# Turning layer 0's attention probabilities in 32 by 32 squares on VectorE, with the squares changing places through DRAM

## The chip, the cores and the metric

The kernel runs on one core of a Trainium2 chip. A core has five engines, each with a queue of its own that is worked through in order: TensorE (matrix products, PE in the profile, with its weight loads as PEld), VectorE (DVE), ScalarE (ACT), GpSimd (POOL) and SyncE (SP). SP and ACT also issue DMAs from their queues (SPq and ACTq in the profile), and 16 DMA engines carry them out. The metric is the device time of one execution in microseconds, the median of several runs.

## The reference

Two decoder layers over 272 tokens (16 learned meta tokens and a sequence of 256), with 16 heads of 128 features. Layer 0 is forgetting attention, layer 1 stick-breaking attention, each with a squared-ReLU MLP behind it. The change is in layer 0's attention:

```python
def forgetting_attention(q, k, v, cum_logf):
    scale = HEAD_DIM ** -0.5
    outs = []
    for qs, qe in query_blocks(q.shape[1]):
        s = jnp.einsum('bqhd,bkhd->bhqk', q[:, qs:qe], k[:, :qe]).astype(jnp.float32) * scale
        s = s + cum_logf[:, :, qs:qe, None] - cum_logf[:, :, None, :qe]
        ...
        p = jax.nn.softmax(s, axis=-1).astype(v.dtype)
        outs.append(jnp.einsum('bhqk,bkhd->bqhd', p, v[:, :qe]))
    return jnp.concatenate(outs, axis=1)
```

The blocks of queries are the 16 meta tokens and two blocks of 128. The softmax runs over keys, and the product with v sums over keys.

## The kernel before

Activations lie feature-major: a feature on a partition, the 272 tokens along the free dimension. Almost all of the time is in `gemm_group`, which computes 512 output features: 16 chunks of 128 input features, four blocks of 128 output features. To keep float32 accuracy at the speed of the float32r type, each operand is split in a high and a low part, and three products (high by high, high by low, low by high) are summed in PSUM. The weights are split on the way: SP loads `raw` blocks (L207), ACT makes the high part `whi` (L218), DVE the low part `wlo` (L219). One weight block is 256 input features by 512; there are four buffers each for `raw`, `whi` and `wlo`, so the splits can run up to four blocks ahead of TensorE, and eight blocks make a group.

In layer 0 the loop at L421 goes over four groups `g` of four heads. Each does three `gemm_group` calls, for q, k and v, and the attention work is woven between the products of the next of these calls:

- L460 to L477: for each head `j`, the scores of both query blocks are computed (L466, and L467 by `by_parts`, L394), added to the decays on DVE (L470), made into exponentials on ACT (L473) and divided by their sums (L475, L477). They stand in `s`, queries on partitions, keys along the free dimension: 144 keys for the first block of queries, 272 for the second.
- L479 to L489: the same for the meta tokens, in `s0`.
- L492 to L507: to be summed over keys, the probabilities must have the keys on partitions. For each pair of heads `pr`, and each head `i` in it, three squares of 128 by 128 are turned on TensorE (L501, a product with the identity), into the PSUM tile `pp`. Two of them are split into a high and a low part `p0` (`split`, L376 on ACT and L377 on DVE), the third goes to `p1` whole (L506).
- L510 to L517: two more squares, the corners `pk_sm` (packed on POOL, L412) and `s0`, are turned on TensorE (L511, L512) and copied to `pm_sb`.
- L519: the `gemm_group` of v. Then v is turned to token-major (`token_major`, L384), and the products with p follow: `weighted` (L397, whose products are at L394) for `p0` and L539 for `p1`.

Each engine's order is made when the program is built: the framework lays the instructions of a queue in an order by a simulated timeline (the argument at L865), and puts a semaphore wait wherever an instruction uses what another engine or a DMA makes. `placed_behind` only pins one instruction behind another on TensorE. An engine whose next instruction waits does nothing else, and that holds for a DMA issue too: an issue on ACT's queue that waits holds up the activations behind it.

The tiles `raw`, `q2` and `p0` of the attention come from three buffers named `pp` in the pool `att`; `p1` shares two buffers of the pool `tmp`.

The kernel already has one trip through DRAM on ACT's queue: in group 0 the forget gates' running sums go to `f_dram` (L370), and are read back from there as `fqm_sb` (L372) and, once in every group, `fk` (L445).

Of the kernel before, what the change touches and what calls it, by code (L numbers as in the profile page):

```python
# [9 lines left out]
F32 = mybir.dt.float32  # L10
# [5 lines left out]
P = 128  # L16
# [17 lines left out]
def yoco_kernel(ctx: ExitStack, tc: tile.TileContext, hT_in, gains, b_f, w_f, w_qkv0, w_o0, w_up, w_dn,  # L34
                w_kv, w_q1, w_o1, g_row, out):
    nc = tc.nc
# [8 lines left out]
    att = ctx.enter_context(tc.tile_pool(name="att", bufs=2))  # L45
    pacc = ctx.enter_context(tc.tile_pool(name="pacc", bufs=4, space=bass.MemoryType.PSUM))
    patt = ctx.enter_context(tc.tile_pool(name="patt", bufs=4, space=bass.MemoryType.PSUM))
# [14 lines left out]
    ident = const.tile([P, P], F32, name="ident")  # L62
# [117 lines left out]
    def placed_behind(product, *others):  # L180

        for o in others:
            tc.add_manual_dep(product.ins, o.ins.name, mybir.DependencyInfo(mybir.DependencyClass.NoSync,
                                                                            mybir.DependencyReason.DATA))
# [136 lines left out]
    fq_sb = const.tile([P, 2, NC], F32, name="fq_sb")  # L321
    fqm_sb = const.tile([P, 4], F32, name="fqm_sb")
    f_dram = tc.dram_tile([NC, T], F32, name="f_dram")

    def load_gates():
        nc.scalar.dma_start(bf_sb, b_f)

        wf_sb = att.tile([P, NC, NC], F32, tag="v_sb", name="wf_sb")
        wf = att.tile([P, NC, 2 * NC], F32, tag="v_sb", name="wf")
        nc.scalar.dma_start(wf_sb, w_f)  # L330
        nc.vector.memset(wf[:, :, NC:], 0.0)
        nc.vector.tensor_tensor(out=wf[:, :, :NC], in0=wf_sb, in1=g_sb[:, G_A0, :].unsqueeze(2).to_broadcast([P, NC, NC]), op=ALU.mult)
        both = att.tile([P, P], F32, tag="pk", name="both")[:, :32]
        nc.vector.tensor_tensor(out=both, in0=ident[:, :32], in1=ident[:, 32:64], op=ALU.add)
        for i in (2, 3):
            nc.vector.tensor_tensor(out=both, in0=both, in1=ident[:, 32 * i:32 * i + 32], op=ALU.add)
        both = both[:, :NC]
        return wf, both
# [35 lines left out]
    def split(hl, src):  # L374

        nc.scalar.activation(hl[:, 0], src, AF.Copy)  # L376
        nc.vector.tensor_tensor(out=hl[:, 1], in0=src, in1=hl[:, 0].bitcast(F32), op=ALU.subtract)  # L377

    def token_major(vT, pr, t0, label):

        pv = patt.tile([P, 2, 2, P], F32, tag="patt", name=f"pv_{label}")
        for i in range(2):
            for b in range(2):
                nc.tensor.transpose(pv[:, i, b, :], vT[:, 2 * pr + i, t0 + b * P:t0 + b * P + P], ident)  # L384
        v0 = att.tile([P, 2, 2, P], F32R, tag="v_sb", name=f"v0_{label}")
        v1 = tmp.tile([P, T], F32, tag="u2", name=f"v1_{label}")[:, :2 * P].rearrange("p (i d) -> p i d", i=2)
        split(v0, pv[:, :, 0, :])
        nc.scalar.copy(v1, pv[:, :, 1, :])
        return v0, v1

    def by_parts(out, a, b, start, stop=False):

        for k, (i, j) in enumerate(((0, 0), (0, 1), (1, 0))):
            product = nc.tensor.matmul(out, a[i], b[j], start=start and k == 0, stop=stop and k == 2)  # L394
        return product

    def weighted(po, v0, p0, i):  # L397

        return by_parts(po[:, i, :], [v0[:, k, i, :] for k in range(2)], [p0[:, k, i, :] for k in range(2)], i == 0)

    def packed(src, label):

# [12 lines left out]
    def put_split(sp, h, nh, t, n, src):  # L415
        hi, lo = (x[:, h:h + nh, t - sp.t0:t - sp.t0 + n] for x in (sp.hi, sp.lo))
        nc.scalar.activation(hi, src, AF.Copy)
        nc.vector.tensor_tensor(out=lo, in0=src, in1=hi.bitcast(F32), op=ALU.subtract)

    ao = Split("o0", 0)  # L420
    for g in range(4):  # L421
# [24 lines left out]
        s = att.tile([P, 4, 416], F32, tag="s", bufs=1, name=f"s_{g}")  # L446
# [15 lines left out]
        for j in range(4):  # L462
            h = 4 * g + j
            ps = patt.tile([P, 512], F32, tag="patt", name=f"ps_{h}")
# [14 lines left out]
        ps = patt.tile([P, 512], F32, tag="patt", name=f"ps0_{g}")  # L479
# [11 lines left out]

        pps = []  # L492
        for pr in range(2):
            p0 = att.tile([P, 2, 2, 256], F32R, tag="pp", bufs=3, name=f"p0_{g}_{pr}")
            p1 = tmp.tile([P, T], F32, tag="relu", name=f"p1_{g}_{pr}")[:, :2 * P].rearrange("p (i q) -> p i q", i=2)
            last = None
            for i in (1, 0):
                j = 2 * pr + i
                pp = patt.tile([P, 512], F32, tag="patt", name=f"pp_{4 * g + j}")
                for b, o in ((2, 144 + P), (1, 144), (0, 0)):  # L500
                    product = nc.tensor.transpose(pp[:, b * P:(b + 1) * P], s[:, j, o:o + P], ident)  # L501
                    if last is not None:
                        placed_behind(product, last)
                    last = product
                split(p0[:, :, i, :], pp[:, :2 * P])
                nc.vector.tensor_copy(p1[:, i, :], pp[:, 2 * P:3 * P])  # L506
            pps.append((p0, p1))  # L507


# [18 lines left out]
        po = patt.tile([P, 512], F32, tag="patt", name=f"pom_{g}")  # L528
# [5 lines left out]
        for pr in range(2):  # L534
            (v0, v1), (p0, p1) = token_major(vT, pr, 0, f"0_{g}_{pr}"), pps[pr]
            po = patt.tile([P, 2, 256], F32, tag="patt", name=f"po0_{g}_{pr}")
            for i in range(2):
                weighted(po, v0, p0, i)
                nc.tensor.matmul(po[:, i, P:], v1[:, i, :], p1[:, i, :], start=False, stop=i == 1)  # L539
            ends = po.rearrange("p i (c q) -> p (i c) q", c=2)[:, :, P - M:]  # L540
            nc.vector.tensor_tensor(out=ends, in0=ends, in1=own[:, 4 * pr:4 * pr + 4], op=ALU.add)
            put_split(ao, 4 * g + 2 * pr, 2, M, S, po)
# [78 lines left out]
    for g in range(4):  # L621
        kT = att.tile([P, 4, T], F32, tag="kT", bufs=1, name=f"kT1_{g}")
        gemm_group(w_kv[2 * g], xc, 0, lambda m, acc: evac_kv(m, acc, kT))
        q = qT1[g]
# [33 lines left out]
        for pr in range(2):  # L658
# [3 lines left out]
            for i in range(2):  # L662
                j = 2 * pr + i
                product = by_parts(pa[:, i, :], [k0[:, k, j, :] for k in range(2)],
                                   [x[:, 4 * g + j] for x in (ao.hi, ao.lo)], True, True)
            for i in range(2):
                j = 2 * pr + i
# [26 lines left out]
            product = nc.tensor.matmul(pb[:, :, :144], ntri_r, e_lo[:, :, 256:400], start=False, stop=True)  # L694
# [8 lines left out]
        ps = []  # L703
        for pr in range(2):
            zp = z[:, 2 * pr:2 * pr + 2, :400]
            nc.scalar.activation(zp, zp, AF.Exp)
            p0 = att.tile([P, 4, T], F32R, tag=("kT", "qT")[pr], bufs=(1, 4)[pr], name=f"p01_{g}_{pr}")
            p0 = p0.rearrange("p h t -> p (h t)")[:, :1024].rearrange("p (a i q) -> p a i q", a=2, i=2)
# [11 lines left out]
        for pr in range(2):  # L720
            v0, v1 = token_major(vT, pr, 0, f"1_{g}_{pr}")
            po = patt.tile([P, 2, 256], F32, tag="patt", name=f"po1_{g}_{pr}")
            for i in range(2):
                j = 2 * pr + i
                product = weighted(po, v0, ps[pr], i)
                if j == 0:
                    placed_behind(nc.tensor.matmul(pv[:, P:P + 64], vc_sb, zc, start=True, stop=True), product)
                    nc.scalar.copy(own, pv[:, P:P + 64].rearrange("p (h q) -> p h q", h=4))
                nc.tensor.matmul(po[:, i, 112:], v1[:, i, :], z[:, j, 256:400], start=False, stop=i == 1)  # L729
            nc.vector.tensor_tensor(out=po[:, :, 240:], in0=po[:, :, 240:], in1=own[:, 2 * pr:2 * pr + 2], op=ALU.add)  # L730
            put_split(ao, 4 * g + 2 * pr, 2, M, S, po)
# [141 lines left out]
```

## Time and profile before

| | |
|---|---|
| median of 3 runs | 2289.8 us (2289.29 to 2289.85) |
| the profiled execution, its own time | 2290.0 us |
| its span in the profile | 2288.3 us |
| granted TensorE clock | 1.0 throughout |
| layer 0's attention, groups 0 to 3 | about 24 to 341 us of the span |
| one group of four heads, groups 1 to 3 | 79.30 us each |
| transposes L501 | 48, 270 to 273 ns each |

A row of a timeline has the start and the length in microseconds, the engine, the line of the kernel, the operation, what it writes and reads, and how many instructions it merges; idle time of the engine before it stands in brackets with what ended it. A row of the stretches has, for each engine, the busy time and the number of instructions, then the granted clock, the DMA engines' busy share and what they moved. A row of DMA issues ends with the size of one transfer and the median time from issue to landing.

### The profile page before, as it was taken

To read this page: it belongs to the slowest core of one execution; us is meant where nothing else is said; L and a number is where in the kernel's file an instruction comes from. 1 tells how busy PE (TensorE), PEld (TensorE's weight loads), DVE (VectorE), ACT (ScalarE), POOL (GpSimd) and SP (SyncE) were. 2 spreads that over 40 slices of the span, in tenths; PEclk is the share of its full clock that TensorE was granted. 3 is DMA by queue.
4 is the path that set the end of the run, shared out by engine and by line. 5 is a ranking of instruction groups with operands and counts; after the bars stand their busy time and mean duration, and the time that the engine had idled before them with its cause. 6 is when DMAs were issued, how large, how long until landed. Compare 5 with 4: busy or idle time off the path is not lost.

```text
span 2288.3 us, 44927 instructions
## 1 busy us (share of the span) xinstructions
PE 2281.3 (100%) x18994; PEld 2272.9 (99%) x18994; DVE 1321.5 (58%) x1858; ACT 1066.4 (47%) x1479; POOL 44.7 (2%) x72
## 2 busy tenths in 40 slices
PE   9999999999999999999999999999999999999999
PEld 9999999999999999999999999999999999999998
DVE  7666565654455455455566666666555555555555
ACT  6444444444354344344444455555543543544554
POOL 1010000000000000000000000000000000000001
PEclk9999999999999999999999999999999999999999
DMA  7545545555555555555555544456556566565564
GB/s 242 171 162 162 181 156 171 175 185 176 180 170 184 180 171 185 175 184 176 174 187 191 177 148 148 154 174 203 186 192 201 186 195 203 185 202 192 186 201 142
DMA packets 116283, 412.60 MB, mean 180 GB/s; under 512 B 13537, under 2 KB 15473, under 8 KB 116081
## 3 DMA queue, kind: packets, MB, share of 16 engines
q1 hardware_dynamic: 113760, 406.29, 54.8%
q10 hardware_dynamic: 2320, 3.43, 0.4%
q8 instruction: 149, 2.44, 0.4%
q14 instruction: 54, 0.43, 0.1%
HBM read 407.55 MB, written 2.11 MB: 179 GB/s over the span
## 4 chain that ended last, share of the span: by engine, by line
PE 99%; DMA 0%; ACT 0%; DVE 0%; issue 0%; POOL 0%; POOLq 0%; SPq 0%; DVEq 0%
PE acc L188 96%; PE po L394 0%; PE pv L384 0%; PE ps L394 0%; PE pza L394 0%; PE pp L501 0%; DMA raw<-w_qkv 0%; PE pzb L668 0%; PE po L729 0%; PE ps L466 0%; PE po L539 0%; DMA hT<-hT_in 0%; ACT whi L218 0%; PE pf L345 0%; DVE wlo L219 0%
## 5 line engine op out<-in xcount | busy, mean ns | idle before, releaser
L219 DVE TENSOR_TENSOR wlo<-raw,whi 128x1024 fp32r<-128x1024 f32 (+1 forms) x773 | 929.1, 1218 | 728.9 <-ACT whi L218 721.8
L218 ACT ACTIVATE whi<-raw 128x1024 fp32r<-128x1024 f32 (+1 forms) x773 | 796.8, 1050 | 978.4 <-PE acc L188 931.4
L188 PE MATMUL acc<-x_m,whi 128*128 128x272 f32 (+1 forms) x4096 | 643.2, 282 | 0.0
L188 PE MATMUL acc<-x_u,whi 128*128 128x272 f32 (+1 forms) x3968 | 626.1, 282 | 0.0
L188 PEld LDWEIGHTS acc<-x_m,whi 128*128 128x128 f32 x4096 | 566.0, 188 | 0.1
L188 PEld LDWEIGHTS acc<-x_u,whi 128*128 128x128 f32 x3968 | 550.3, 188 | 0.0
L188 PE MATMUL acc<-x_m,wlo 128*128 128x272 f32 (+1 forms) x2048 | 441.3, 282 | 0.0
L188 PE MATMUL acc<-x_u,wlo 128*128 128x272 f32 (+1 forms) x1984 | 432.0, 282 | 0.0
L188 PE MATMUL acc<-x_a,whi 128*128 128x272 f32 (+1 forms) x2048 | 357.5, 286 | 0.0
L188 PEld LDWEIGHTS acc<-x_m,wlo 128*128 128x128 f32 x2048 | 323.5, 188 | 0.0
L188 PEld LDWEIGHTS acc<-x_u,wlo 128*128 128x128 f32 x1984 | 315.3, 188 | 0.0
L188 PEld LDWEIGHTS acc<-x_a,whi 128*128 128x128 f32 x2048 | 301.8, 189 | 1.6 <-ACT whi L218 0.7
L188 PE MATMUL acc<-x_a,wlo 128*128 128x272 f32 (+1 forms) x1024 | 254.4, 286 | 0.1
L188 PE MATMUL acc<-x_kv,whi 128*128 128x272 f32 x1024 | 193.1, 288 | 0.0
L188 PEld LDWEIGHTS acc<-x_a,wlo 128*128 128x128 f32 x1024 | 175.8, 189 | 0.8 <-DVE ssq_a L158 0.4
L188 PE MATMUL acc<-x_o,whi 128*128 128x272 f32 (+1 forms) x1024 | 162.8, 282 | 0.0
L188 PEld LDWEIGHTS acc<-x_kv,whi 128*128 128x128 f32 x1024 | 160.4, 189 | 0.1
L188 PE MATMUL acc<-x_kv,wlo 128*128 128x272 f32 x512 | 147.6, 288 | 0.0
L188 PEld LDWEIGHTS acc<-x_o,whi 128*128 128x128 f32 x1024 | 142.4, 188 | 0.0
L300 DVE TENSOR_TENSOR hT<-acc,hT 128x272 f32<-128x272 f32 (+1 forms) x156 | 67.3, 431 | 75.5 <-PE acc L188 75.3
L188 PE MATMUL acc<-x_o,wlo 128*128 128x272 f32 (+1 forms) x512 | 110.9, 283 | 0.0
L188 PEld LDWEIGHTS acc<-x_kv,wlo 128*128 128x128 f32 x512 | 96.6, 189 | 0.0
(253 smaller groups left out, 1084.8 us busy)
## 6 DMA issues: line engine op xcount, KB each, us to landing
raw<-w_up SPq DMA_DIRECT2D x256, 512.0 KB, 4.4
raw<-w_dn SPq DMA_DIRECT2D x256, 512.0 KB, 4.3
raw<-w_qkv SPq DMA_DIRECT2D x92, 512.0 KB, 3.8
raw<-w_o SPq DMA_DIRECT2D x64, 512.0 KB, 4.2
raw<-w_kv SPq DMA_DIRECT2D x64, 512.0 KB, 4.1
raw<-w_q SPq DMA_DIRECT2D x32, 512.0 KB, 4.6
fk<-f_dram ACTq DMA_DIRECT2D x4, 544.0 KB, 4.8
raw<-w_qkv SPq DMA_DIRECT2D x7, 256.0 KB, 4.7
```

The source lines that it names most:

```text
L188: ins = nc.tensor.matmul(*args, **kw).ins
L218: on_act = nc.scalar.activation(hp, src, AF.Copy)
L219: on_dve = nc.vector.tensor_tensor(out=lp, in0=src, in1=hp.bitcast(F32), op=ALU.subtract)
L300: nc.vector.tensor_tensor(out=hT[:, c, t0:], in0=acc, in1=hT[:, c, t0:], op=ALU.add)
```

## The change

TensorE no longer turns layer 0's probabilities. For each pair of heads:

1. DVE turns each square of 128 by 128 as sixteen squares of 32 by 32, each in its place (six instructions), from `s` into a new float32 tile `raw`. After this the squares stand right inside, but those that belong on other partitions are still on the old ones: square (a, c) of the block stands at partitions 32a and columns of c, and belongs at partitions 32c and columns of a.
2. Four DMAs on ACT's queue write the four rows of squares (32 partitions each, pieces of 192 float32) to the scratch `p_dram[pr]` in DRAM.
3. Two DMAs on ACT's queue read them back with the squares in their places: 64 float32 a piece into `raw` (what becomes `p0`), and 32 a piece into `p1`. Each has 128 partitions of 8 pieces.
4. One `split` of 512 columns makes `p0` out of `raw`; there is no copy to `p1`.

The columns of `p0` and `p1` now stand in another order, and the products L394 and L539 read them through a view in runs of 32 columns. In layer 1 only the way in which `weighted` is handed its operand is rewritten. `raw` takes buffers of the three named `pp`.

```diff
+    p_dram = [tc.dram_tile([4, 32, 4, 192], F32, name=f"p_dram_{i}") for i in range(2)]
...
-        return by_parts(po[:, i, :], [v0[:, k, i, :] for k in range(2)], [p0[:, k, i, :] for k in range(2)], i == 0)
+        return by_parts(po[:, i, :], [v0[:, k, i, :] for k in range(2)], [p0[k][i] for k in range(2)], i == 0)
...
+            raw = att.tile([P, 2, 2, 256], F32, tag="pp", bufs=3, name=f"raw_p0_{g}_{pr}").rearrange("p x i q -> p (x i q)")
             p0 = att.tile([P, 2, 2, 256], F32R, tag="pp", bufs=3, name=f"p0_{g}_{pr}")
             p1 = tmp.tile([P, T], F32, tag="relu", name=f"p1_{g}_{pr}")[:, :2 * P].rearrange("p (i q) -> p i q", i=2)
-            last = None
-            for i in (1, 0):
-                j = 2 * pr + i
-                pp = patt.tile([P, 512], F32, tag="patt", name=f"pp_{4 * g + j}")
-                for b, o in ((2, 144 + P), (1, 144), (0, 0)):
-                    product = nc.tensor.transpose(pp[:, b * P:(b + 1) * P], s[:, j, o:o + P], ident)
-                    if last is not None:
-                        placed_behind(product, last)
-                    last = product
-                split(p0[:, :, i, :], pp[:, :2 * P])
-                nc.vector.tensor_copy(p1[:, i, :], pp[:, 2 * P:3 * P])
+
+            y = raw[:, :768].rearrange("p (c h b i) -> p c h b i", c=4, h=2, b=3)
+            for i in range(2):
+                for b, o in enumerate((0, 144, 144 + P)):
+                    nc.vector.transpose(y[:, :, i, b, :], s[:, 2 * pr + i, o:o + P].rearrange("p (c k) -> p c k", c=4))
+            y = y.rearrange("p c h b i -> p c (h b i)")
+            for a in range(4):
+                nc.scalar.dma_start(p_dram[pr].rearrange("c j a x -> a j c x")[a], y[32 * a:32 * a + 32])
+            back = p_dram[pr].rearrange("c j a (h x) -> (c j) (a h) x", h=2)
+            raw = raw[:, :512]
+            nc.scalar.dma_start(raw.rearrange("p (m x) -> p m x", m=8), back[:, :, :64])
+            nc.scalar.dma_start(p1.rearrange("p i q -> p (i q)").rearrange("p (m x) -> p m x", m=8), back[:, :, 64:])
+            p0 = p0.rearrange("p x i q -> p x (i q)")
+            split(p0, raw)
+
+            p0 = p0.rearrange("p x (a h b i) -> p x h b a i", a=4, h=2, b=2)
+            p0 = [[p0[:, k, i] for i in range(2)] for k in range(2)]
+            p1 = p1.rearrange("p i q -> p (i q)").rearrange("p (a h i) -> p h a i", a=4, h=2)
             pps.append((p0, p1))
...
-                nc.tensor.matmul(po[:, i, P:], v1[:, i, :], p1[:, i, :], start=False, stop=i == 1)
+                nc.tensor.matmul(po[:, i, P:], v1[:, i, :], p1[:, i], start=False, stop=i == 1)
...
-                product = weighted(po, v0, ps[pr], i)
+                product = weighted(po, v0, [[ps[pr][:, k, h, :] for h in range(2)] for k in range(2)], i)
```

## The prediction

> **What bounds the kernel now.** I read the page first: engine totals, the chain that ended last, the queues.
>
> ```profile
> span 2288.3 us, 44927 instructions
> PE 2281.3 (100%) x18994; PEld 2272.9 (99%) x18994; DVE 1321.5 (58%) x1858; ACT 1066.4 (47%) x1479; POOL 44.7 (2%) x72
> PE 99%; DMA 0%; ACT 0%; DVE 0%; issue 0%; POOL 0%; POOLq 0%; SPq 0%; DVEq 0%
> q1 hardware_dynamic: 113760, 406.29, 54.8%
> q10 hardware_dynamic: 2320, 3.43, 0.4%
> ```
>
> TensorE is never idle for long and 99% of the chain is its own work. So every pass taken off it shortens the kernel by its pitch, and everything else costs nothing until TensorE has to wait for it. Next came the stage that the change touches: busy time by stretch, for one head group of layer 0 (groups 1 to 3 have the same period, 79.30 us) and for two stretches in which its softmax ends.
>
> ```profile
> core 0: us, PE busy (x) PEld busy (x) DVE busy (x) ACT busy (x) POOL busy (x), PEclk, DMA share, GB/s
> 103.44:182.74 79.30, 79.30 (x648) 79.30 (x648) 49.63 (x98) 35.95 (x61) 6.34 (x6) 1.00 0.51 167
> 147.00:151.00 4.00, 4.00 (x35) 4.00 (x33) 4.00 (x11) 3.45 (x10) 1.42 (x2) 1.00 0.38 125
> 151.00:155.00 4.00, 4.00 (x36) 4.00 (x35) 2.80 (x8) 2.02 (x5) 0.00 (x0) 1.00 0.75 241
> ```
>
> TensorE works all 79.30 us; VectorE and ScalarE have room over the group, but for four microseconds VectorE is full.
>
> **What is removed.** Twelve transposes a group, 48 in all. Their price is not the 273 ns that one lasts but the pitch at which TensorE goes on. The timeline of group 1 (start, length, engine) has runs of three and of six; then come a piece of the chain that is ordinary products alone, and the tile's own view with the rest of what goes:
>
> ```profile
> 146.02 0.29 PE L188 MATMUL acc<-x_a,whi 128*128 128x272 f32 x1
> 146.14 0.49 PE L501 MATMUL pp<-ident,s 128*128 128x128 f32 x3
> ...
> 146.60 0.29 PE L188 MATMUL acc<-x_a,wlo 128*128 128x272 f32 x1
> 151.51 0.69 PEld L501 LDWEIGHTS pp<-ident,s 128*128 128x128 f32 x6
> 152.17 0.14 PEld L511 LDWEIGHTS pm<-ident,pk_sm 128*128 128x128 f32 x1
> ...
> 103.44 34.42 PE acc L188 x279
> ...
> L501 PE MATMUL pp<-ident,s x48: 270/273/273, 74.0 to 310.8; 128*128 128x128 f32 x48
> L376 ACT ACTIVATE p<-pp x16: 358/369/384, 74.9 to 311.1; 128x256 fp32r<-128x256 f32 x16
> L377 DVE TENSOR_TENSOR p<-pp,p x16: 396/412/424, 75.6 to 311.7; 128x256 fp32r<-128x256 f32 x16
> L506 DVE COPY p<-pp x16: 272/279/282, 75.9 to 312.0; 128x128 f32<-128x128 f32 x16
> ```
>
> Six weight loads take 152.17 - 151.51 = 0.66 us, 0.11 each. Three transposes and two ordinary products take 0.58 us from 146.02 to 146.60; an ordinary product is 0.123 (34.42 us for 279), so the three cost 0.333, 0.111 each. 48 x 0.111 = **5.3 us** off TensorE. Per group ScalarE loses 4 x 0.37 = 1.5 us and VectorE 4 x (0.41 + 0.28) = 2.8 us.
>
> [...]
>
> **What is added on VectorE and ScalarE.** Twelve 32x32-square transposes of 128x128 a group. The trace has none. Bounds from the rows below: 0.19 us (a copy of 128x32) and 0.43 (128x272); I take 0.28, the copy of 128x128 that goes. That is 3.4 us (2.3 to 5.2). Two splits of 128x512 replace four of 128x256: 0.63 each on ScalarE, 0.68 on VectorE.
>
> ```profile
> 52.87 0.19 DVE L368 COPY fq_sb<-pfq 128x32 f32<-128x32 f32 x1 [1.48 <-PE pfq L367]
> 65.09 0.43 DVE L470 CUSTOM_DVE_ANT_0 s<-ps,s 128x272 f32<-128x272 f32 x1
> 40.92 0.63 ACT L376 ACTIVATE q<-qT 128x512 fp32r<-128x512 f32 x1 [0.22 <-DVE qT L427]
> L377 DVE TENSOR_TENSOR q<-qT,q 128x512 fp32r<-128x512 f32 x4 | 2.7, 682 | 0.0
> ```
>
> VectorE nets +2.0 us a group (0.9 to 3.8), ScalarE -0.2. Neither is on the path while the weight splits keep ahead (below).
>
> **The trip through DRAM.** Each pair of heads issues four writes and two reads on ScalarE's queue, 12 a group. The reads wait until the writes have landed, the split until the first read has; while ScalarE's queue waits, every activation behind it waits too: the next weight block's high part (L218), the exponentials of later heads (L473, L487), later copies. The kernel has one such trip already, the forget gates in group 0:
>
> ```profile
> 49.07 1.06 ACT L218 ACTIVATE whi<-raw 128x1024 fp32r<-128x1024 f32 x1 [0.66 <-PE acc L188]
> 50.05 0.34 ACTq L370 DMA_DIRECT2D f_dram<-fc  x1
> 52.32 2.79 ACTq L372 DMA_DIRECT2D fqm_sb<-f_dram  x4
> ...
> 55.68 0.43 ACT L417 ACTIVATE x_o<-kT 128x272 fp32r<-128x272 f32 x1 [5.54 <-DMA fqm_sb<-f_dram]
> 56.02 1.04 ACT L218 ACTIVATE whi<-raw 128x1024 fp32r<-128x1024 f32 x1
> 50.00:56.00 6.00, 6.00 (x50) 5.83 (x49) 2.32 (x5) 0.46 (x2) 0.00 (x0) 1.00 0.49 158
> ...
> fk<-f_dram ACTq DMA_DIRECT2D x4, 544.0 KB, 4.8
> f_dram<-fc ACTq DMA_DIRECT2D x1, 17.0 KB, 2.2
> ```
>
> Here ScalarE stood for 5.54 us and gave out no weight block from 49.07 to 56.02, and TensorE worked 6.00 of 6.00 us. Why: a weight block lasts TensorE about 2.96 us, and there are four buffers.
>
> ```profile
> 156.96 1.06 ACT L218 ACTIVATE whi<-raw 128x1024 fp32r<-128x1024 f32 x1 [1.97 <-issue]
> 159.92 1.06 ACT L218 ACTIVATE whi<-raw 128x1024 fp32r<-128x1024 f32 x1 [1.90 <-PE acc L188]
> 161.01 1.23 DVE L219 TENSOR_TENSOR wlo<-raw,whi 128x1024 fp32r<-128x1024 f32 x1 [1.73 <-ACT whi L218]
> ```
>
> A split starts when its buffer comes free and is needed three blocks later: 3 x 2.96 = 8.9 us, less 1.06 and 1.23, leaves **6.6 us** by which it may be late. One pair's trip costs ScalarE 4 x 0.34 = 1.4 us of write issues, 2.2 for the landing (bounds 2.2 and 4.8), 2 x 0.5 = 1.0 for the reads' issue (0.34 as the gates' write to 2.79 / 4 = 0.70 as their reads), 2.2 to 4.8 for their landing. A read has 1024 pieces of 256 or 128 bytes where a gate read has 128; if the issue grew with the pieces it would take 8 x 0.70 = 5.6 us, the outer bound that I keep for the range. Whole and with nothing put between, a pair takes 6.8 to 9.4 us, near the limit, but group 0's gap of 6.95 us was free. The planner that orders each engine's instructions can put other work into the waits, since ScalarE is busy only 35.95 of 79.30 us. So I take **0** for it; the price without this cover stands under the starving rival.
>
> Other queues: SP carries only the raw loads, which wait for L219 to free a buffer, so a late split makes them late too, by no more than the split. VectorE's half of a p0 split waits for ScalarE's, with the next L219 behind it: the same lateness and the same 6.6 us. p1 comes by DMA straight to where TensorE reads it, with nothing on an engine behind it.
>
> Is p0 in time? VectorE ends the last scaling of a head group, then POOL copies corners and TensorE turns the two small squares that stay:
>
> ```profile
> 148.54 0.56 DVE L477 TENSOR_SCALAR s<-s,st 128x144 f32<-128x144 f32 x2
> 148.96 1.42 POOL L412 COPY pk_sm<-s 128x64 f32<-128x64 f32 x2 [31.76 <-DVE s L477]
> 177.08 0.40 PE L394 MATMUL po<-p,v 128*128 128x256 f32 x2
> 178.13 0.39 PE L539 MATMUL po<-p,v 128*128 128x128 f32 x2
> 68.35 0.38 PE L480 MATMUL ps<-kT,pk_qm 128*128 128x128 f32 x2
> ...
> L394 PE MATMUL po<-p,v x6: 281/284/365, 177.1 to 178.6; 128*128 128x256 f32 x6
> ```
>
> The probabilities exist at 149.1 and are first used at 177.08: 28 us of cover for two trips of 10 us and their splits. Cost 0.
>
> The load on the 16 DMA engines: 4 x 128 + 1024 + 1024 = 2560 pieces and 0.79 MB a pair. By bytes, at q1's 406.29 MB in 54.8% of 2288.3 us (324 KB/us), 2.4 us; by pieces, at q10's 0.4% x 2288.3 x 16 / 2320 = 63 ns, 10 us. Two pairs add 6% to 25% of the group to a share of 0.51: still under 1, and raw weights are loaded four blocks ahead. Cost 0.
>
> **The new reading pattern.** TensorE now reads p0 and p1 in runs of 32 columns. The squares' product L480 reads runs of 32 in float32, and its two passes take 0.38 us, as L539's two over whole rows take 0.39. For float32r no row has such runs: bounds 0, and one more pass each, 12 a group at 0.12 (L394's pair: 0.40 - 0.28), 48 x 0.12 = 5.8 us in all. I take 0, as L480 says.
>
> **Sum**, for the profiled execution: 2290.0 us with 1.7 outside the span; 2290.0 - 5.3 = 2284.7. It was 0.2 above the median of 2289.8, so **2284.5** for the median.
>
> **The rivals.**
> *Starving* (slower). The planner leaves a pair's trip whole on ScalarE, and a weight split stands behind it: 1.4 + 2.2 + 1.0 + 4.8 + 0.63 = 10.0 us late, 3.4 more than 6.6; four groups lose 13.6 us: 2298.1. Both trips back to back are 20.0, 13.4 too many a group: 2338. It decides from a lateness of 6.6 us on. For it: landings under load were 4.8, and many small pieces are untried. Against: group 0's stand. [...]
> *Small squares late* (no change). Write issues and one landing, 1.4 + 2.2 = 3.6 us, stand ahead of an exponential; POOL's corners, ready at 150.4, are used at 152.17, so 1.8 is covered and 1.8 a group lost: 7.2, 2291.7. VectorE's full stretch at 147 to 151 speaks for it; that the writes can only follow the first pair's scaling, with few exponentials left, against.
> *Reading in runs of 32 costs a pass* (no change): 2284.5 + 5.8 = 2290.3. L480 speaks against.
> *More comes off than the pitch* (faster): if a transpose held TensorE for its whole 0.273, 13.1 us, 2276.7. The pitch speaks against. That the change leaves the transposes on TensorE is excluded by its code.
>
> **How the numbers follow.** A measurement here tells about 0.2% (4.6 us) from no change. Forecast 0.46 (own range 2283.8 to 2285.2); more comes off 0.03; reading pattern 0.07; small squares late, or a loss of one or two microseconds of any kind, 0.15; starving 0.29. Faster 0.49, same 0.22, slower 0.29. The range 2283.5 to 2306 leaves out the larger gain and the worse half of starving.
>
> **What would show it.** No transposes L501, twelve square transposes on VectorE at about 0.28 us each; group periods of 78.0 us instead of 79.30; po L394 pairs still 0.40; reads on ScalarE's queue issued over 2 us after the last write; no idle TensorE before L188 released by a weight split. I am wrong if TensorE idles for L218 or L219 (starving) or before L511 and L512 (small squares), or if L394's pitch is near 0.24.

## The result and the profile after

The changed kernel takes 2297.2 us (median of 7 runs, 2292.89 to 2301.04) against 2289.7 for the kernel before on the same chip (7 runs, 2289.29 to 2290.89). The ratio is 1.0033 with an interval of 1.0021 to 1.0044: it is slower, where the prediction said 2284.5. The profiled execution of after was its longest, 2301.04 us, so the profile shows the loss at its largest: its span is 11.0 us over the 2288.3 of before.

Lines of the kernel after are meant from here on: up to the change they are one higher than before, behind it nine (so L432 evacuates the accumulators of v, L378 makes the low half of a split, L505 writes, L508 and L509 read, L502 turns the squares). First the page of after: span, engine totals, the chain's shares.

```profile
span 2299.3 us, 44921 instructions
PE 2282.9 (99%) x18946; PEld 2272.6 (99%) x18946; DVE 1326.4 (58%) x1882; ACT 1065.7 (46%) x1471; POOL 45.1 (2%) x72
PE 95%; DMA 3%; ACT 0%; issue 0%; DVE 0%; ACTq 0%; POOL 0%; SPq 0%; POOLq 0%; DVEq 0%
```

The 48 transposes are gone (18994 products became 18946). Yet 3% of the chain that ends last is now a DMA, and a chain that was 99% TensorE is 95%. The engines' totals look as before; only the chain says that somebody waits. Where is it? The stretches of the four head groups, first of before for group 0 (the other three were 79.30 each), then of after:

```profile
24.00:103.44 79.44, 79.44 (x653) 77.03 (x652) 57.80 (x118) 41.03 (x76) 3.29 (x6) 1.00 0.55 179
```

```profile
24.00:104.53 80.53, 78.80 (x643) 76.17 (x642) 59.05 (x125) 40.73 (x75) 1.38 (x6) 1.00 0.64 197
104.53:188.03 83.50, 80.44 (x637) 79.69 (x637) 50.91 (x105) 35.90 (x59) 6.34 (x6) 0.98 0.57 178
188.03:270.10 82.07, 80.20 (x636) 79.67 (x636) 51.07 (x104) 35.84 (x59) 5.20 (x6) 0.98 0.58 180
270.10:352.33 82.23, 79.97 (x637) 79.48 (x636) 50.91 (x105) 35.97 (x59) 5.21 (x6) 0.98 0.59 180
```

The groups lose 1.09, 4.20, 2.77 and 2.93 us: 11.0 together, so the whole loss lies in the four stretches that the change touches. Two things are new in them. TensorE idles (period less busy time) for 1.73, 3.06, 1.87 and 2.26 us, 8.9 in all. And in three groups its granted clock is 0.98 over the stretch. What it waits for is in the view of waits, first of TensorE, then of all engines (total, times, longest):

```profile
PE acc L188 <- DVE vT L432: 7.1, 4, 2.4
PE pvm L533 <- POOL pk_vm L406: 1.9, 3, 0.6
```

```profile
ACT p L377 <- DMA raw_p<-p_dram: 26.9, 7, 8.2
DVE p L378 <- ACT p L377: 26.8, 9, 6.7
```

TensorE does not wait for weight splits, as the starving rival had it, but for VectorE to empty the accumulators of v, once in each group. VectorE's own wait is for ScalarE, and ScalarE's for the read from DRAM. The timeline of VectorE in group 1 puts the two together:

```profile
157.76 0.69 DVE L378 TENSOR_TENSOR p<-raw_p,p 128x512 fp32r<-128x512 f32 x1 [1.23 <-ACT p L377]
160.46 2.36 DVE L219 TENSOR_TENSOR wlo<-raw,whi 128x1024 fp32r<-128x1024 f32 x2 [2.01 <-DMA raw<-w_qkv]
162.73 0.78 DVE L432 TENSOR_TENSOR vT<-acc,rstd_a 128x272 f32<-128x272 f32 x2
170.21 0.69 DVE L378 TENSOR_TENSOR p<-raw_p,p 128x512 fp32r<-128x512 f32 x1 [6.70 <-ACT p L377]
170.82 0.78 DVE L432 TENSOR_TENSOR vT<-acc,rstd_a 128x272 f32<-128x272 f32 x2
```

In before nothing stood between the second and the third evacuation (L431 there); the third waited only for the products:

```profile
164.43 0.44 DVE L431 TENSOR_TENSOR vT<-acc,rstd_a 128x272 f32<-128x272 f32 x1 [1.04 <-PE acc L188]
```

In VectorE's order of after the low half of pair 1's split (L378) stands between the second and the third of the four evacuations of v. It waits 6.70 us, and two finished accumulators that need no more than 0.4 us each stay full behind it. TensorE, which has work for other accumulators up to 168.88, then stops:

```profile
168.59 0.29 PE L188 MATMUL acc<-x_a,wlo 128*128 128x272 f32 x1
171.31 0.52 PE L188 MATMUL acc<-x_a,whi 128*128 128x272 f32 x2 [2.43 <-DVE vT L432]
172.94 0.33 PE L533 MATMUL pvm<-ident,pk_vm 128*128 128x128 f32 x1 [0.62 <-POOL pk_vm L406]
```

The second stop, 0.62 us, is the same lateness once more: POOL can pack v's corners only after the last evacuation.

Why is the split so late? The chain that ended last, followed within that stretch of after, has pieces of DMA where there were only products before:

```profile
150.41 6.66 DMA raw_p<-p_dram
...
157.09 0.32 ACT p L377
...
158.42 4.00 DMA p_dram<-raw_p
...
162.59 6.88 DMA raw_p<-p_dram
...
169.55 0.64 ACT p L377
```

ScalarE's timeline has the four writes between the first two of these:

```profile
157.10 2.11 ACTq L505 DMA_DIRECT2D p_dram<-raw_p  x4
```

The two trips run one behind the other. Pair 1's writes stand on ScalarE's queue behind pair 0's split, which waits for pair 0's read. And a trip is long: from 157.10 to the end of the split, 169.55 + 0.64 = 170.19, it took 13.1 us, 12.4 of them up to the landing of the read, where the prediction's longest without the split was 9.4. For most of the last read both engines just stand, while the DMA engines are nearly full with raw weights:

```profile
164.00:168.00 4.00, 4.00 (x35) 4.00 (x34) 0.00 (x0) 0.00 (x0) 0.00 (x0) 1.00 0.92 266
```

The prices of the new parts stand in the DMA issues of after (count, size, median us to landing) and in the views of its tiles (ns: smallest, median, largest; the products of layer 0 alone):

```profile
p_dram<-raw_p ACTq DMA_DIRECT2D x32, 96.0 KB, 2.0
raw_p<-p_dram ACTq DMA_DIRECT2D x8, 256.0 KB, 5.8
p<-p_dram ACTq DMA_DIRECT2D x8, 128.0 KB, 6.9
```

```profile
L502 DVE STREAM_TRANSPOSE raw_p<-s x48: 268/272/310, 69.3 to 320.4; 128x128 f32<-128x128 f32 x48
L395 PE MATMUL po<-p,v x48: 278/282/368, 99.0 to 351.8; 128*128 128x256 f32 x48
```

### The profile page after: what moved, and what is told of

Same layout as the page of the kernel before. It is cut to its first block, busy times and chain, and to the rows that moved or that the text cites. A ratio compares the mean times of both kernels' runs of the same rounds, so it can differ in the third digit from the quotient of the medians.

```text
span 2299.3 us, 44921 instructions
## 1 busy us (share of the span) xinstructions
PE 2282.9 (99%) x18946; PEld 2272.6 (99%) x18946; DVE 1326.4 (58%) x1882; ACT 1065.7 (46%) x1471; POOL 45.1 (2%) x72
## 4 chain that ended last, share of the span: by engine, by line
PE 95%; DMA 3%; ACT 0%; issue 0%; DVE 0%; ACTq 0%; POOL 0%; SPq 0%; POOLq 0%; DVEq 0%
PE acc L188 92%; DMA raw_p<-p_dram 2%; DMA p_dram<-raw_p 1%; DMA raw<-w_qkv 1%; PE po L395 0%; PE pv L385 0%; PE ps L395 0%; PE pza L395 0%; ACTq L505 0%; DMA p<-p_dram 0%; PE pzb L677 0%; PE po L738 0%; PE ps L467 0%; POOL pk_vm L406 0%; ACT p L377 0%
## 5 line engine op out<-in xcount | busy, mean ns | idle before, releaser
L219 DVE TENSOR_TENSOR wlo<-raw,whi 128x1024 fp32r<-128x1024 f32 (+1 forms) x773 | 928.8, 1218 | 720.0 <-ACT whi L218 711.6
L218 ACT ACTIVATE whi<-raw 128x1024 fp32r<-128x1024 f32 (+1 forms) x773 | 797.1, 1051 | 953.9 <-PE acc L188 914.7
L188 PE MATMUL acc<-x_m,whi 128*128 128x272 f32 (+1 forms) x4096 | 643.1, 282 | 0.0
L188 PE MATMUL acc<-x_u,whi 128*128 128x272 f32 (+1 forms) x3968 | 626.0, 282 | 0.0
L188 PEld LDWEIGHTS acc<-x_m,whi 128*128 128x128 f32 x4096 | 566.0, 188 | 0.1
L188 PEld LDWEIGHTS acc<-x_u,whi 128*128 128x128 f32 x3968 | 550.4, 188 | 0.0
L188 PE MATMUL acc<-x_m,wlo 128*128 128x272 f32 (+1 forms) x2048 | 440.9, 281 | 0.0
L188 PE MATMUL acc<-x_u,wlo 128*128 128x272 f32 (+1 forms) x1984 | 431.6, 282 | 0.0
L188 PE MATMUL acc<-x_a,whi 128*128 128x272 f32 (+1 forms) x2048 | 359.2, 287 | 6.1 <-DVE vT L432 5.4
L188 PEld LDWEIGHTS acc<-x_m,wlo 128*128 128x128 f32 x2048 | 323.3, 188 | 0.0
L188 PEld LDWEIGHTS acc<-x_u,wlo 128*128 128x128 f32 x1984 | 315.1, 188 | 0.0
L188 PEld LDWEIGHTS acc<-x_a,whi 128*128 128x128 f32 x2048 | 303.7, 190 | 8.3 <-DVE vT L432 6.1
L188 PE MATMUL acc<-x_a,wlo 128*128 128x272 f32 (+1 forms) x1024 | 255.7, 287 | 0.0
L188 PE MATMUL acc<-x_kv,whi 128*128 128x272 f32 x1024 | 193.2, 288 | 0.0
L188 PEld LDWEIGHTS acc<-x_a,wlo 128*128 128x128 f32 x1024 | 177.0, 190 | 0.7 <-DVE ssq_a L158 0.4
L188 PE MATMUL acc<-x_o,whi 128*128 128x272 f32 (+1 forms) x1024 | 164.0, 283 | 1.6 <-DVE vT L432 1.6
L188 PEld LDWEIGHTS acc<-x_kv,whi 128*128 128x128 f32 x1024 | 160.2, 189 | 0.1
L188 PE MATMUL acc<-x_kv,wlo 128*128 128x272 f32 x512 | 147.5, 288 | 0.0
L188 PEld LDWEIGHTS acc<-x_o,whi 128*128 128x128 f32 x1024 | 143.3, 189 | 1.9 <-DVE vT L432 1.9
L188 PE MATMUL acc<-x_o,wlo 128*128 128x272 f32 (+1 forms) x512 | 111.3, 283 | 0.0
L188 PEld LDWEIGHTS acc<-x_kv,wlo 128*128 128x128 f32 x512 | 96.5, 188 | 0.0
```

What stands on the lines that cost most here:

```text
L188: ins = nc.tensor.matmul(*args, **kw).ins
L218: on_act = nc.scalar.activation(hp, src, AF.Copy)
L219: on_dve = nc.vector.tensor_tensor(out=lp, in0=src, in1=hp.bitcast(F32), op=ALU.subtract)
```

## The experiments

Three theories stood after this. **A**, VectorE's order: the time goes where its low half stands ahead of v's evacuations. **B**, ScalarE's stand: it goes where ScalarE stands for the read, as in the prediction's starving rival, and the evacuations are only the last to show it. **C**: what is read in runs of 32, or the load on the DMA engines, costs TensorE time everywhere, without idle time. Open besides: what the removed transposes are worth alone, and whether a shorter read, or one trip instead of two, would do. The first four kernels ran on one chip (before there: 2289.84, 29 runs), the last four on another (2289.97, 28 runs).

**e1: only the low half moves.** Pair 1's low half goes behind v's last evacuation on VectorE; ScalarE's order is that of after.

```diff
-            split(p0, raw)
+            nc.scalar.activation(p0[:, 0], raw, AF.Copy)
+            if pr == 0:
+                nc.vector.tensor_tensor(out=p0[:, 1], in0=raw, in1=p0[:, 0].bitcast(F32), op=ALU.subtract)
+            else:
+                low = (p0, raw)
...
         gemm_group(w_qkv0[3 * g + 2], xa, 0, lambda m, acc: evac_kv(m, acc, vT))
+        placed_behind(nc.vector.tensor_tensor(out=low[0][:, 1], in0=low[1], in1=low[0][:, 0].bitcast(F32),
+                                              op=ALU.subtract), box["evac"])
```

> Only the VectorE half of the second pair's split (p0 low) is moved behind the four evacuations of v's accumulators; ScalarE's queue keeps its order and its long stand at the high half. Theory A (VectorE's queue: the low half stands ahead of the last two evacuations, which free the accumulators that TensorE's next group needs): no idle TensorE before L188, granted clock 1.0 throughout, 2289.7 - 5.3 = 2284.4, up to 2285.5 with small waits. Theory B (ScalarE's stand makes the weight blocks late): nothing better, 2294 to 2300, TensorE idle as before. Theory C (what is read in runs of 32 or the load on the DMA engines costs TensorE time everywhere): about 2297 with no idle.

It measured 2286.9 us (2286.45 to 2287.61), a ratio of 0.9987 (0.9978 to 0.9996): one instruction a group moved on one queue turns the loss into a gain. VectorE's timeline of e1 in group 1, and its row for the tile's wait on ScalarE:

```profile
162.96 0.44 DVE L432 TENSOR_TENSOR vT<-acc,rstd_a 128x272 f32<-128x272 f32 x1 [1.04 <-PE acc L188]
164.44 0.44 DVE L432 TENSOR_TENSOR vT<-acc,rstd_a 128x272 f32<-128x272 f32 x1 [1.04 <-PE acc L188]
167.86 0.69 DVE L533 TENSOR_TENSOR p<-raw_p,p 128x512 fp32r<-128x512 f32 x1 [2.98 <-ACT p L511]
```

```profile
ACT p L511 <- DMA raw_p<-p_dram: 32.5, 8, 7.7
```

ScalarE stands about as long as before the move (32.5 us in 8 waits, the longest 7.7; after has 26.9 in 7 and another 7.3 in one put down to the `p1` read), and the last two evacuations of this group now wait for nothing but the products. B and C fall; A holds, though the time is 1.4 us over the upper end of its range. Of that, one stop of 0.6 us before L188 is left in group 0, and group 2 took 78.51 us where group 1 took 78.13, without idle time.

**e2: both halves of both pairs move**, the high ones behind `vm_sb` on ScalarE, the low ones behind the evacuations on VectorE, so that neither engine stands in front of work.

```diff
-            split(p0, raw)
+            splits.append((p0, raw))
...
+        on_act = nc.scalar.copy(vm_sb, pv[:, :2 * P])
+        for p0, raw in splits:
+            placed_behind(nc.scalar.activation(p0[:, 0], raw, AF.Copy), on_act)
+            placed_behind(nc.vector.tensor_tensor(out=p0[:, 1], in0=raw, in1=p0[:, 0].bitcast(F32), op=ALU.subtract),
+                          box["evac"])
```

> Both halves of both pairs' splits are moved: ScalarE's behind the copy of the small v tiles, VectorE's behind v's evacuations. Neither engine then waits for a read to land early. Theory A and theory B: 2284.4 both, no idle; against the kernel that moves only the low half, A expects no difference above 0.5 us, B expects this one to be 10 us better. Theory C: about 2297.

2286.34 us (2285.65 to 2289.17), ratio 0.9986 (0.9977 to 0.9995). Freeing ScalarE as well adds 0.6 us to what e1 gives, less than the two spreads: what B named was worth next to nothing. Both theories' 2284.4 was too low by 1.9 us.

**e3: a shorter read, order unchanged.** The block is read back in one DMA of 128 pieces of 3072 bytes in place of two of 1024 pieces; VectorE copies the `p1` part out of it. The order of low half and evacuations is left to the framework, as in after.

```diff
-            nc.scalar.dma_start(raw.rearrange("p (m x) -> p m x", m=8), back[:, :, :64])
-            nc.scalar.dma_start(p1.rearrange("p i q -> p (i q)").rearrange("p (m x) -> p m x", m=8), back[:, :, 64:])
+            nc.scalar.dma_start(raw[:, :768], p_dram[pr].rearrange("c j a x -> (c j) (a x)"))
...
+            nc.vector.tensor_copy(p1.rearrange("p i q -> p (i q)").rearrange("p (m y) -> p m y", m=8), back[:, :, 64:])
```

> The two reads of 1024 pieces of 256 and 128 bytes become one of 128 pieces of 3072 bytes; the split then picks its columns, and p1 is copied on VectorE (0.28 us more a pair). If the pieces, taking turns with the weights' packets, made the reads slow: landing about 4 us in place of 5.8 to 6.9, VectorE's wait before the second low half under 4 us in place of 5 to 6.7, TensorE's idle mostly gone, 2284.5 to 2288. If the latency of DRAM or the bytes made it: landing 5.5 to 7 as now, 2295 to 2300. Theory C: about 2297.

The expectation was missed: 2295.97 us (2292.95 to 2298.7), ratio 1.0025 (1.0014 to 1.0036), not to be told from after. The read did land sooner, but the timeline of e3 in group 1 shows a new piece in front of the evacuations:

```profile
166.82 0.29 DVE L509 COPY p<-raw_p 128x256 f32<-128x256 f32 x1 [1.13 <-DMA raw_p<-p_dram]
167.03 0.43 DVE L432 TENSOR_TENSOR vT<-acc,rstd_a 128x272 f32<-128x272 f32 x1
167.47 0.69 DVE L378 TENSOR_TENSOR p<-raw_p,p 128x512 fp32r<-128x512 f32 x1
168.08 1.13 DVE L432 TENSOR_TENSOR vT<-acc,rstd_a 128x272 f32<-128x272 f32 x3
```

```profile
raw_p<-p_dram ACTq DMA_DIRECT2D x8, 384.0 KB, 4.3
```

It lands in 4.3 us instead of 5.8, yet the copy to `p1`, which went to no engine before, waits for the same DMA, and now all four evacuations stand behind the trip instead of two. The profiled execution was the shortest of its seven. Shortening the wait while more stands behind it did not help; e8 below takes the same read with the order mended.

**e6: no trip.** The squares stay on their own partitions: the writes and reads are left out, `p0` is split from what VectorE turned and `p1` copied from it. This leaves out the exchange of squares, so the output is another; what stays is the removed transposes, the added ones, and the work behind them.

> The squares are turned on VectorE but do not change places: no writes, no reads, the split takes them as they stand, and p1 is copied on VectorE; the exchange between partitions is left out. This gives the price of what is taken off TensorE together with the squares on VectorE and the reading in runs of 32. Theories A and B: 2284.4, group periods 77.97 us, clock 1.0. Theory C in its form with the runs of 32: 2290. With a transpose that held TensorE for its whole 0.273 us: 2276.6.

2285.33 us (2284.96 to 2286.6), ratio 0.998 (0.9972 to 0.9989). Its stretch of group 1:

```profile
141.76:219.97 78.21, 78.21 (x636) 78.21 (x635) 51.24 (x107) 35.89 (x59) 4.24 (x6) 1.00 0.53 169
```

79.30 - 78.21 = 1.09 us a group, 4.4 for four. That is what the transposes were worth, not 5.3, and it puts A's 2284.4 0.9 us too low.

**e4 and e5: one pair each.** In e4 pair 0 goes the new way and pair 1 is turned on TensorE as before; in e5 (`pr == 1` in the diff) it is the other way round.

```diff
+            if pr == 0:
                 y = raw[:, :768].rearrange("p (c h b i) -> p c h b i", c=4, h=2, b=3)
...
+            else:
+                last = None
+                for i in (1, 0):
...
```

> Only the first pair of each group goes the new way, the second is turned on TensorE as before. Theory A: the first pair's low half stands well ahead of v's evacuations, so its wait costs nothing: half of the 4.5 us that the kernel without a trip gained, 2289.8 - 2.2 = 2287.6, no idle before L188, clock 1.0 throughout. Were every trip to cost alike: half of the loss too, about 2289.8 - 2.2 + 6 = 2293.6.

> Only the second pair of each group goes the new way. Its low half stands ahead of the last three evacuations of v, but its trip starts sooner than in the changed kernel, since no first pair's split stands before its writes on ScalarE. Theory A: most of the loss stays, idle before L188 after VectorE's evacuation in every group, 2290 to 2297, and at least 2.5 us above the kernel with only the first pair changed. Were every trip to cost alike: 2293.6, the same as that kernel.

e4 took 2292.23 us (2291.35 to 2293.25), ratio 1.0009 (1.0 to 1.0018), where a gain was expected; e5 2288.94 (2288.0 to 2290.49), ratio 0.9996 (0.9987 to 1.0004). Both expectations of theory A were missed: e5 was to be the slower by 2.5 us at least, and is the faster by 3.3. So A names the right queue, but what it said of where, and how late, a single trip strikes was wrong. e4 lost its time in group 0 alone (77.69 us from its first meta product to that of group 1, 74.33 before): 1.8 us of it are idle time, and one stretch of 3.41 us at half the clock follows (last section). Its timelines of VectorE and TensorE there:

```profile
83.32 0.44 DVE L432 TENSOR_TENSOR vT<-acc,rstd_a 128x272 f32<-128x272 f32 x1 [1.04 <-PE acc L188]
87.97 0.69 DVE L378 TENSOR_TENSOR p<-raw_p,p 128x512 fp32r<-128x512 f32 x1 [4.21 <-ACT p L377]
...
89.64 0.78 DVE L432 TENSOR_TENSOR vT<-acc,rstd_a 128x272 f32<-128x272 f32 x2
```

```profile
88.92 0.29 PE L188 MATMUL acc<-x_a,wlo 128*128 128x272 f32 x1
90.12 0.52 PE L188 MATMUL acc<-x_a,whi 128*128 128x272 f32 x2 [0.92 <-DVE vT L432]
```

It is the same pattern with one trip, with one difference: between the two last rows VectorE works for 1.1 us on pair 1's splits and copies, which come from TensorE in e4 and stand behind the same wait. Without them the last two evacuations would have begun 1.1 us sooner, and the stop is only 0.92; so e4's loss is not that of the trip alone. The rows give the margin. The third evacuation was due 1.48 us behind the second (the spacing of e1's rows), at 84.80, and done at 85.24; TensorE ran on until 88.92 + 0.29 = 89.21. So an evacuation of v may be **4.0 us** late. In after the third one began at 170.82; e1, whose group starts 1.52 us earlier (142.36 against 143.88), has it at 162.96, so it was due at 164.5 and 6.3 late: 2.3 over the margin, against a measured stop of 2.43.

In e5 the one trip begins early, since no other stands in front of it; reckoned from the group's start its low half in group 1 runs 3.2 us sooner than after's (164.71 - 141.62 against 170.21 - 143.88), and TensorE waits for evacuations of v 0.4 us in two waits over the whole kernel. e4 and e5 together would be 1.2 us over before; both changes in one kernel are 6.2 over it (the repeat below, on the same chip). So the loss isn't a price for each pair: most of it comes only when both trips stand on one queue, the second behind the first. One thing stays open: six transposes fewer should be worth half of 1.09 us a group, but e4's groups 1 and 2 gain 0.11 (79.19) with no idle time, and their ordinary products were slower (576 of them 72.69 us from start to start in group 1, 72.32 before). Why, no run shows.

**e8: whole rows, both halves and the copy behind.** e2's order with e3's read.

> Whole rows of 3072 bytes in one read, and both halves of the splits, with the copies to p1, behind v's evacuations. Theory A: as the kernel with both halves behind, 2285.3 (the kernel without a trip) to 2286.3; the shorter landing has nothing left to win but the load on the DMA engines.

2284.94 us (2284.57 to 2285.28), ratio 0.9977 (0.9969 to 0.9986): the lowest median of all, below both kernels and a little below the expected range, with the smallest spread. Its stretch of group 1:

```profile
141.24:219.40 78.16, 78.16 (x637) 78.16 (x635) 51.19 (x107) 35.55 (x59) 5.47 (x6) 1.00 0.60 189
```

No idle time, full clock, 1.14 us less than before in a group, and 11.3 us less over the whole than the kernel after on the same chip.

**after_again: the kernel after without an edit**, beside e4, e5 and e8.

> The changed kernel once more on the same chip as the others: 2293 to 2301, median about 2297; in its profile idle before L188 after VectorE's evacuation in all four groups, and the granted clock at 0.5 for some 3.4 us after it in the groups where a second idle of 0.6 us (waiting for GpSimd's packing) follows.

2296.2 us (2292.73 to 2298.47), ratio 1.0026 (1.0014 to 1.0038), as the first time. Its profile shows TensorE's waits for L432 again, 6.7 us in four. Half the clock followed in two of the three groups with a second stop of 0.6 us, not in all three as expected.

## Why the prediction was wrong

**The step that failed** reads: "VectorE's half of a p0 split waits for ScalarE's, with the next L219 behind it: the same lateness and the same 6.6 us." Behind the second pair's half the next instruction is not L219 but L432, an evacuation of v. Its margin is 4.0 us (e4), and it was 6.3 us late, which would still have been in time for a weight split. The prediction asked how late a weight split may come, and gave that answer to the whole queue. Moving this one instruction (e1) took 10.3 us off (2297.2 to 2286.9, on two chips whose kernel before differs by 0.2).

**The trip's length** was the second error. Bounds were 6.8 to 9.4 us for a pair without its split; the second one of group 1 took 12.4. The 9.4 left out the prediction's own upper bound for the landing of the writes: with 4.8 in place of 2.2 it comes to 12.0. By terms: from the first write's issue to the landing of the last 157.10 to 162.42, 5.3 us (1.4 + 2.2 were taken); the read 6.88 (at most 4.8); the split as priced, the reads' issue 1.2 (1.0). The read's bound came from a transfer in 128 pieces; this one has 1024. With one piece a partition it landed in 4.3 (e3), though it moved half as much again. That the two pairs would queue up was considered, at 20.0 us for both, but only for the weight splits. Those never starved: VectorE and ScalarE gave out weight blocks between the waits, and TensorE's waits for L218 come to 0.6 us in the whole of after.

**"Is p0 in time?"** was answered rightly, and to the wrong question: no product L395 waited for `p0` in after. The 28 us of cover are there for the data; the instruction that makes the data has no such cover, since what stands behind it in its queue has only 4.0.

**The removal** was mis-sized by a sixth: 5.3 us predicted from a pitch of 0.111, 4.4 measured in e6 (1.09 / 12 = 0.091 each) and 4.6 in e8. In the trace of before the twelve of group 1 take 1.15 us from start to start, 0.095 each; the prediction's two short pieces of timeline gave too much.

**What was right.** The squares on VectorE take 0.272 us (0.28 taken). The products over runs of 32 columns cost nothing: L395's median in layer 0 is 282 ns where L394's was 283, and the twelve of group 1 take 1.66 us from start to start in e6, 1.67 before. The DMA engines had room: groups 1 to 3 rose from a share of 0.51 to 0.57 to 0.59. And the sum, were the wait not there, is 2284.5 against the 2284.94 of e8 and 2285.33 of e6; the difference is about what the removal was over-priced by. So the parts were priced well, and the order was not looked at.

**The starving rival**, at 2298.1, had the time nearly right by luck, with another mechanism: the lateness is that of ScalarE's long stand, but it is not the weight splits that it strikes. The small squares (L511 and L512 of before) made no stop.

**What the sum had no term for** is the clock. Of the 11.0 us of the profiled run 8.9 are idle time, and the half-clock stretches of groups 1 to 3 (last section), with 3.41, 3.42 and 2.95 us of work in them, cost an estimated half of that, 4.9; less the 4.4 saved leaves 9.4. The other 1.6 us aren't accounted for.

## What to carry to other kernels

When a change puts a wait on an in-order engine, list what stands behind the waiting instruction in that engine's order, up to the end of the wait, and find the margin of each; the smallest counts, not that of the commonest. A long latency is hidden for the data when its consumer is far away, but for the queue only if the waiting instruction is placed late, just before its consumer: here that one placement was worth more than twice the change itself (10.3 us against 4.4). Two round trips on one queue are to be costed as a sum where the second's issues stand behind the first's wait, as here (the first's read landed at 157.07, the second's writes were issued from 157.10 on); the other order no run tried.

## What the runs showed of the hardware

**Half the clock after some stops of TensorE.** In groups 1 to 3 of after the profile shows three stretches with the granted clock at 0.50, from 173.30, 255.22 and 337.14 us on, each 3.41 us long, with 81.92 us from the start of one to that of the next. The rows below are such a stretch and the 3.41 us ahead of it; for group 0 of after and group 2 of the repeat, which have none, they are cut 81.92 us away from those of the next or the previous group. First after, group 0 and group 1:

```profile
87.97:91.38 3.41, 1.68 (x15) 1.46 (x13) 1.39 (x3) 1.46 (x2) 0.55 (x3) 1.00 0.50 110
91.38:94.80 3.42, 3.42 (x30) 3.42 (x29) 2.42 (x3) 2.51 (x4) 0.10 (x1) 1.00 0.43 82
169.89:173.30 3.41, 1.37 (x9) 1.15 (x10) 3.09 (x5) 2.19 (x3) 1.63 (x2) 1.00 0.00 0
173.30:176.72 3.42, 3.41 (x16) 3.09 (x16) 0.66 (x1) 0.93 (x2) 0.94 (x2) 0.50 0.78 261
```

Then the repeat, group 1 and group 2, and group 0 of e4:

```profile
167.31:170.73 3.42, 1.68 (x12) 1.25 (x10) 2.26 (x4) 2.52 (x3) 0.81 (x1) 1.00 0.07 11
170.73:174.14 3.41, 2.94 (x13) 2.89 (x14) 1.49 (x2) 0.37 (x1) 1.76 (x3) 0.50 0.57 175
249.23:252.65 3.42, 1.92 (x14) 1.48 (x12) 2.26 (x4) 2.53 (x3) 0.81 (x1) 1.00 0.03 6
252.65:256.06 3.41, 2.54 (x19) 2.33 (x20) 1.49 (x2) 0.85 (x2) 1.76 (x3) 1.00 0.57 172
```

```profile
88.97:92.39 3.42, 1.88 (x13) 1.45 (x13) 3.42 (x8) 1.40 (x2) 1.91 (x2) 1.00 0.00 0
92.39:95.80 3.41, 3.18 (x15) 2.86 (x14) 0.38 (x1) 1.14 (x2) 0.66 (x2) 0.50 0.79 273
```

After a stretch with 1.37, 1.68 or 1.88 us of work in 3.41 (2.0, 1.7 and 1.5 us idle) the next ran at half the clock, with 13 to 16 products against the 30 of group 0's at full clock; after 1.92 it didn't, and after the 1.68 of group 0 it didn't either, so busy time alone does not sort these rows. The number of products does: 9, 12 and 13 of them were followed by half the clock, as were 11, 11 and 8 in groups 2 and 3 of after and group 3 of the repeat; 14 and 15 were not. That was seen afterwards, and no run tests it or shows what lies behind it. After's seven runs spread over 8.2 us, with a mean granted clock of 0.997 in the longest and 0.999 in the shortest; e8's eleven, with no stop for an evacuation in the profile, spread over 0.7. How much of the difference is the clock's was not tried by itself.

**Small pieces beside a heavy stream.** The read of 1024 pieces took 5.8 us in the median, and 6.9 in group 1 of after, where the DMA engines were 0.92 busy for most of it, for 256 KB that at the 266 GB/s of that stretch would be 1 us; 128 pieces of 3072 bytes with 384 KB landed in 4.3 in e3. No run changed the size of the pieces and nothing else.
